# High and low parts side by side in the inputs of two feed-forward layers

## The chip, the core and the metric

The kernel runs on one core of one Trainium2 chip. The metric is the device time of one execution in microseconds (us); lower is better. Engines carry the profile's names: PE is TensorE's matmul, PEld its weight load, DVE is VectorE, ACT ScalarE, POOL GpSimd, SP SyncE. In a matmul the stationary side is loaded into the array first (a LDWEIGHTS, shown under PEld), and the moving side then streams past it; the number of moving columns is the last number of a row's 128x512.

## The reference

A decoder trunk of two layers over 256 positions of width 2048, all in float32. Cut to what matters here:

```python
D_MODEL, SEQ, DEPTH = 2048, 256, 2
D_FF = (8 * D_MODEL + 3 * 256 - 1) // (3 * 256) * 256      # 5632

def rms_norm(x, g):
    xf = x.astype(jnp.float32)
    y = xf * lax.rsqrt(jnp.mean(xf * xf, axis=-1, keepdims=True) + NORM_EPS)
    return (y * g.astype(jnp.float32)).astype(x.dtype)

def swiglu(x, w_gate, w_up, w_down):
    return (jax.nn.silu(x @ w_gate) * (x @ w_up)) @ w_down

def reference(x, ...):
    for layer in range(DEPTH):
        xn = rms_norm(x, norm_mix[layer])
        if layer % 2 == 0:
            x = x + mixer_mlstm_ssd(xn, *mixer_params[layer])
        else:
            x = x + mixer_moba(xn, *mixer_params[layer])
        x = x + swiglu(rms_norm(x, norm_ffn[layer]), *ffn_params[layer])
    return rms_norm(x, final_norm)
```

The change touches the input of `swiglu` in both layers, and nothing of the two mixers.

## The kernel before

**Precision.** A matmul takes float32r operands. To keep float32 accuracy each operand is split into a high part (the value rounded to float32r) and a low part (what is left over), and a product of two operands is three matmuls: high by high, high by low, low by high (`add`, L470 to L474).

**Activations.** A `KT` (L256) holds one activation matrix, transposed: 2048 features are 16 k-tiles of 128, in four blocks of four k-tiles, each block a tile `[P, 4, 2, T]` of 128 partitions, four k-tiles, high and low, and 256 positions. So the high part of a k-tile is a run of 256 values of four bytes, and its low part the next run. `parts(k)` gives the two views, `both(k)` both as one run of 512 columns, which only the strips of `lin_w` use as a moving side. `x1` and `x3` are the inputs of the feed-forward layers, `x2` that of the attention; `normed_later` (L924) makes all three. The gain of the norm is folded into the split (`turned`, L286): PE transposes 128 x 128 pieces of the residual into PSUM, ACT writes the high part and DVE the low part. The norm's factor per position is put in after the matmuls.

**Weights.** `weights` (L427) loads the rows of one pair of k-tiles, 128 x 2 x 512 values from each of two sources, and splits them: ACT writes `wh`, DVE subtracts and writes `wl`.

**Strips.** `block` (L456) computes 256 positions by two strips of 512 columns; for gate and up one strip of each. It walks the 16 k-tiles as eight pairs, in an order that a plan gives, a letter for each pair. At a `P` it issues the plain product: four outputs (two halves of the positions by two strips), two k-tiles, three matmuls, 24 in all. At an `S` the pair, seen as a 2 x 2 block matrix, goes by a scheme with seven products in place of eight (21 matmuls), for which sums and differences of weights (`sums`, `sh`, `sl`) and of activations (`kt.sums`, made by `activation_sums`, L308) are needed. The activation sums are split into high and low too; their tiles are `skx`, `[P, 4, 2, P]`, four sums of 128 positions. In all these matmuls the activations (128 positions of a k-tile or of a sum) are the stationary side and the 512 weight columns the moving one.

**The feed-forward layer.** `ffn` (L992) handles its 5632 hidden columns as 11 strips in groups of 4, 4 and 3. For each strip `hidden` runs a `block` of gate and up over `x1` or `x3`; the first strip's plan is `PLAN_LATE`, PPPSPSPP, that of the others `PLAN_X`, PSPSPSPP. The hidden values are transposed and split into a `KT` `ha` or `hb`, and after each group `add_blocks` multiplies them by the down weights and adds them to the residual. So each value of `x1` and `x3` is written once and loaded by 11 strips, the values of `ha` and `hb` by the two column halves of one down product.

**Order.** A tile framework sets semaphores and puts instructions in order by priority; nothing in it depends on the step of an operand. All weights come through the SP queue, 512 KB at a time.

Of the kernel before, what the change touches and what calls it, by code (L numbers as in the profile page):

```python
# [9 lines left out]
F32 = mybir.dt.float32  # L10
F32R = mybir.dt.float32r
# [6 lines left out]
P = 128  # L18
T = 256
NT = T // P  # L20
D = 2048
KD = D // P
# [43 lines left out]
def hybrid_trunk(ctx: ExitStack, tc: tile.TileContext, a: dict, out: bass.AP):  # L66
    nc = tc.nc
# [83 lines left out]
    def small(shape, name, dt=F32):  # L151
        return res.tile(shape, dt, tag="small", name=name, bufs=PLAN_X.count("S"))
# [103 lines left out]
    class KT:  # L256


        def __init__(self, name, n, home=blk):
            self.name, self.blocks, self.home, self.sums = name, [None] * (n // 4), home, {}  # L260

        def block(self, b):
            if self.blocks[b] is None:
                self.blocks[b] = self.home([P, 4, 2, T], f"{self.name}{b}", F32R)
            return self.blocks[b]

        def parts(self, k):
            need((self.name, k // 4))
            b = self.block(k // 4)
            return b[:, k % 4, 0, :], b[:, k % 4, 1, :]  # L270

        def both(self, k):
            need((self.name, k // 4))
# [10 lines left out]
            turned(kt, b, pt.rearrange("p (a b) -> p a b", a=2), gcol, half)  # L284

    def turned(kt, b, pair, gcol, half):  # L286
        blk_ = kt.block(b)
        ks = slice(2 * half, 2 * half + 2)
        summed = 2 * b + half in kt.sums
        if summed:  # L290
            xg = t2([P, 2, T], "xg")
            if gcol is None:
                nc.scalar.copy(xg, pair)
            else:
                for j in range(2):
                    c = gcol + 4 * b + 2 * half + j
                    nc.scalar.activation(xg[:, j, :], pair[:, j, :], AF.Copy, scale=pv[:, c:c + 1])
            split(blk_[:, ks, 0, :], blk_[:, ks, 1, :], xg)
            kt.sums[2 * b + half] = activation_sums(xg, gcol is not None)
        elif gcol is None:  # L300
            split(blk_[:, ks, 0, :], blk_[:, ks, 1, :], pair)
        else:
            for j in range(2):
                k = 2 * half + j
                split(blk_[:, k, 0, :], blk_[:, k, 1, :], pair[:, j, :],
                      pv[:, gcol + 4 * b + k:gcol + 4 * b + k + 1])

    def activation_sums(a, gains):  # L308

        a11, a12, a21, a22 = a[:, 1, :P], a[:, 0, :P], a[:, 1, P:], a[:, 0, P:]  # L310
        sf = t2([P, 4, P], "sf")
        nc.vector.tensor_add(sf[:, 0, :], a21, a22)
        nc.vector.tensor_sub(sf[:, 2, :], a11, a21)
        nc.vector.tensor_sub(sf[:, 1, :], sf[:, 0, :], a11)
        nc.vector.tensor_sub(sf[:, 3, :], a12, sf[:, 1, :])
        if gains:
            sk = small([P, 4, 2, P], "skx", F32R)
        else:
            sk = held_tile("skh", [P, 4, 2, P], "skh", F32R)
        split(sk[:, :, 0, :], sk[:, :, 1, :], sf)  # L320
        return sk

    def sums_of(kt, j):

        need((kt.name, j // 2))
        pair = kt.block(j // 2)[:, 2 * (j % 2):2 * (j % 2) + 2, :, :]
        xg = t2([P, 2, T], "xg")
        nc.vector.tensor_add(xg, pair[:, :, 0, :].bitcast(F32), pair[:, :, 1, :].bitcast(F32))
        kt.sums[j] = activation_sums(xg, True)

    def transpose_later(kt, b, src, gcol, wait, step=1):
        for half in range(2):
# [123 lines left out]
    def block(src, kt, row, nk, plan, after_sums=None, lead=1, pairs=None, ahead=()):  # L456

        n = nk // 2
        pairs = pairs[:plan.count("S")] if pairs else [j for j in range(n) if plan[j] == "S"]
        rest = [j for j in range(n) if j not in pairs]
        order = [(pairs if kind == "S" else rest).pop(0) for kind in plan]
        F = [None] * 4
        pre = None
        E = {}

        def add(dst, a, b, start, stop):  # L470
            (ah, al), (bh, bl) = a, b
            nc.tensor.matmul(dst, ah, bh, start=start, stop=False)  # L472
            nc.tensor.matmul(dst, ah, bl, start=False, stop=False)  # L473
            nc.tensor.matmul(dst, al, bh, start=False, stop=stop)  # L474

        first_s, last_s = plan.find("S"), plan.rfind("S")
        turn["aux"] = 0
        group = []
        for i_, j in enumerate(order):
            for when, fn, *args in ahead:  # L480
                if when == i_:
                    fn(*args)
            for i in range(i_, min(i_ + 3, n)):
                if plan[i] == "S" and order[i] not in kt.sums:
                    sums_of(kt, order[i])
            if plan[i_] == "S":
                held[0] = True
                wh, wl, sh, sl = weights(src, row + 2 * j * P, True)
                tok = lambda k, t: tuple(x[:, t * P:(t + 1) * P] for x in kt.parts(k))
                k2, k1 = 2 * j, 2 * j + 1  # L490
                a11, a12, a22 = tok(k1, 0), tok(k2, 0), tok(k2, 1)
                sk = kt.sums[j]
                s1, s2, s3, s4 = [(sk[:, i, 0, :], sk[:, i, 1, :]) for i in range(4)]
                b21, b11, b22 = [(wh[:, i, :], wl[:, i, :]) for i in range(3)]
                t3, t1, t2_, t4 = [(sh[:, i, :], sl[:, i, :]) for i in range(4)]
                prod = {1: (a11, b11), 2: (a12, b21), 3: (s4, b22), 4: (a22, t4),
                        5: (s1, t1), 6: (s2, t2_), 7: (s3, t3)}
                for p in (2, 3, 1, 7, 5, 6, 4):
                    if p in (2, 3, 4):
                        i = p - 2  # L500
                        add(F[i], *prod[p], start=False, stop=False)
                    else:
                        if p not in E:
                            E[p] = bank({1: 4, 7: 5, 5: 6, 6: 7}[p], "acc_e")
                        add(E[p], *prod[p], start=i_ == first_s, stop=i_ == last_s)
                if i_ == last_s:
                    pre = [t2([P, STRIP], "pre") for _ in range(4)]
                    p1, v, u3, w = pre
                    with tc.high_priority(offset=1600 if lead == 1 else 400):
                        nc.scalar.copy(p1, E[1])  # L510
                        nc.vector.tensor_add(v, p1, E[6])
                        nc.vector.tensor_add(u3, v, E[7])
                        nc.vector.tensor_add(v, v, E[5])
                        nc.vector.tensor_add(w, u3, E[5])
                        if after_sums is not None:
                            after_sums(pre)
            else:
                group.append((j, weights(src, row + 2 * j * P, False)))
                if len(group) < lead and i_ < n - 1 and n - i_ <= lead:
                    continue  # L520
                for i in range(4):
                    t, s = divmod(i, 2)
                    first = F[i] is None
                    if first:
                        F[i] = bank(i, "acc_f")
                    for cut in halved if len(group) == lead == 2 and i == 3 else (slice(0, STRIP),):
                        for jj, (wh, wl) in group:
                            for kk in range(2):
                                xh, xl = kt.parts(2 * jj + kk)
                                ts = slice(t * P, (t + 1) * P)  # L530
                                add(F[i][:, cut], (xh[:, ts], xl[:, ts]), (wh[:, 2 * s + kk, cut], wl[:, 2 * s + kk, cut]),
                                    start=first and jj == group[0][0] and kk == 0,
                                    stop=jj == order[-1] and kk == 1 and cut.stop == STRIP)
                group = []
            tick()
            if i_ == last_s:
                held[0] = False
        return F, pre
# [384 lines left out]

    def normed_later(name, gcol, waits=((2, 1), (2, 1), (1, 0), (2, 0))):  # L924

        nx = KT("x" + name, KD, long)
        nx.sums = summed(PLAN_X)
        ss = cst.tile([P, NT, 4], F32, name="ss" + name)

        def finish(s):  # L930
            cs = slice(s * STRIP, (s + 1) * STRIP)
            transpose_later(nx, s, [xr_[t][:, cs] for t in range(NT)], gcol, *waits[s])
            for t in range(NT):
                sumsq(ss[:, t, s:s + 1], xr_[t][:, cs])

        return nx, ss, finish
# [260 lines left out]
```

## Time and profile before

| | |
|---|---|
| Time, median of 2 runs | 2580.02 us (2579.95 to 2580.09) |
| Span of the profiled execution, first to last instruction | 2578.2 us |
| Matmuls, and as many weight loads | 12222 |
| Moved by DMA | 496.55 MB, 193 GB/s on average |
| Groups that read `x` as stationary side in `block`: L472, L473, L474 on acc_f | 1122 matmuls each |

The profile is one execution, taken by the hardware's profiler. Its page lists busy time by engine, the span in 40 slices, the DMA queues, the chain of work that ended last, and the costliest groups of instructions: source line, engine, operation, written tile, read tiles, shape, count, then busy time in us, mean duration in ns, and the idle time of the engine just before them with what ended it. The durations of matmuls overlap, since they are pipelined and their ends are modelled (a row of 390 ns can follow another by 227 ns), so distances are taken from start to start. In the view of the order in time a row has the start in us, the duration, the engine, and at its end how many equal instructions it stands for. In the view of one tile a row has minimum, median and maximum duration in ns, then the first and the last start in us.

### The profile page before, as it was taken

What the parts mean: (1) busy time and instruction counts of PE and PEld (TensorE: products, weight loads), DVE (VectorE), ACT (ScalarE), POOL (GpSimd) and SP (SyncE); (2) the same over time, 40 slices, a digit from 0 to 9 for tenths busy, and PEclk for the clock granted to TensorE, in tenths of its full rate; (3) what the DMA queues carried; (4) which work ended last, traced back from release to release, by engine and by line L of the source; (5) the groups of instructions that cost most, each with busy time, mean ns of one, the idle gap of its engine ahead of it and who ended that gap; (6) DMA issues with size and microseconds to landing.
All of it is one profiled execution on the core that took longest, in us unless ns stands there. A gap on an engine that the chain in (4) does not pass through costs nothing.

```text
span 2578.2 us, 32660 instructions
## 1 busy us (share of the span) xinstructions
PE 2563.5 (99%) x12222; PEld 2130.7 (83%) x12222; DVE 2196.5 (85%) x2831; ACT 1454.3 (56%) x1929; POOL 43.6 (2%) x77
## 2 busy tenths in 40 slices
PE   9999999999999999999999999999999999999998
PEld 8888888888888888888888888888888888888887
DVE  6676777799989998899889986767999888988898
ACT  6465665566665554555455665666655545554554
POOL 2000010000000000000000000000000000000000
PEclk9999999999999999999999999999999999999999
DMA  7566576566564656465656556554555655565554
GB/s 237 170 211 182 166 235 182 163 205 212 185 213 163 215 194 212 163 226 188 206 167 225 186 174 229 164 180 146 180 192 200 212 181 199 193 213 191 199 188 154
DMA packets 254767, 496.55 MB, mean 193 GB/s; under 512 B 15704, under 2 KB 16608, under 8 KB 254352
## 3 DMA queue, kind: packets, MB, share of 16 engines
q1 hardware_dynamic: 250384, 483.26, 57.1%
q0 software_dynamic: 2896, 8.51, 1.1%
q10 hardware_dynamic: 1328, 2.70, 0.3%
q8 instruction: 96, 1.57, 0.2%
q14 instruction: 63, 0.52, 0.1%
HBM read 492.26 MB, written 2.14 MB: 192 GB/s over the span
## 4 chain that ended last, share of the span: by engine, by line
PE 90%; DVE 5%; issue 2%; DMA 2%; ACT 1%; SPq 0%; POOL 0%; POOLq 0%; DVEq 0%; ACTq 0%
PE acc_f L473 18%; PE acc_f L474 18%; PE acc_f L472 17%; PE acc_w L381 11%; PE acc_w L385 5%; PE acc_e L472 4%; PE acc_e L473 4%; PE acc_e L474 4%; PE acc_a L412 2%; PE acc_a L413 2%; PE acc_a L411 2%; DVE wl L441 2%; PE p_tr L282 2%; PE p_y L866 1%; DMA raw<-in_l_w_o 1%
## 5 line engine op out<-in xcount | busy, mean ns | idle before, releaser
L439 ACT CAST wh<-raw 128x1024 fp32r<-128x1024 f32 (+1 forms) x577 | 630.0, 1134 | 412.9 <-PE acc_f L474 338.1
L441 DVE TENSOR_TENSOR wl<-raw,wh 128x1024 fp32r<-128x1024 f32 (+1 forms) x577 | 748.7, 1323 | 79.1 <-ACT wh L439 73.8
L474 PE MATMUL acc_f<-wh,x 128*128 128x512 f32 x1122 | 438.2, 391 | 0.0
L473 PE MATMUL acc_f<-wl,x 128*128 128x512 f32 x1122 | 437.5, 390 | 0.1
L472 PE MATMUL acc_f<-wh,x 128*128 128x512 f32 x1122 | 436.5, 391 | 0.0
L366 DVE TENSOR_TENSOR wl<-raw,wh 128x1024 fp32r<-128x1024 f32 (+1 forms) x225 | 271.3, 1218 | 139.8 <-ACT wh L365 137.3
L439 ACT CAST wh<-sums 128x1024 fp32r<-128x1024 f32 x222 | 227.9, 1051 | 225.9 <-PE acc_f L474 137.7
L365 ACT CAST wh<-raw 128x1024 fp32r<-128x1024 f32 (+1 forms) x225 | 231.9, 1044 | 196.3 <-PE acc_w L381 111.6
L441 DVE TENSOR_TENSOR wl<-sums,wh 128x1024 fp32r<-128x1024 f32 x222 | 266.7, 1221 | 34.6 <-ACT wh L439 34.1
L473 PEld LDWEIGHTS acc_f<-wl,x 128*128 128x128 f32 x1122 | 210.7, 188 | 44.9 <-DVE wl L441 1.9
L474 PEld LDWEIGHTS acc_f<-wh,x 128*128 128x128 f32 x1122 | 210.7, 188 | 43.1
L472 PEld LDWEIGHTS acc_f<-wh,x 128*128 128x128 f32 x1122 | 210.6, 188 | 42.6
L381 PE MATMUL acc_w<-xa,wh 128*128 128x512 f32 x768 | 207.5, 398 | 1.5 <-DVE xa L229 1.5
L381 PEld LDWEIGHTS acc_w<-xa,wh 128*128 128x128 f32 x768 | 138.8, 189 | 27.9 <-DVE xa L229 1.6
L448 DVE TENSOR_TENSOR sums<-raw 128x1024 f32<-128x1024 f32 x111 | 135.4, 1220 | 12.9 <-DMA raw<-in_l_ffn_up 8.0
L381 PE MATMUL acc_w<-x,wh 128*128 128x512 f32 x512 | 138.9, 399 | 0.0
L385 PE MATMUL acc_w<-xa,wl 128*128 128x256 f32 x768 | 121.8, 282 | 0.0
L385 PEld LDWEIGHTS acc_w<-xa,wl 128*128 128x128 f32 x768 | 110.1, 190 | 6.7
L474 PE MATMUL acc_f<-wh,hb 128*128 128x512 f32 (+1 forms) x284 | 109.6, 387 | 0.0
L473 PE MATMUL acc_f<-wl,hb 128*128 128x512 f32 (+1 forms) x284 | 109.6, 387 | 0.0
L472 PE MATMUL acc_f<-wh,hb 128*128 128x512 f32 (+1 forms) x284 | 109.5, 387 | 0.0
L472 PE MATMUL acc_f<-wh,ha 128*128 128x512 f32 x280 | 109.0, 390 | 0.0
(362 smaller groups left out, 4581.3 us busy)
## 6 DMA issues: line engine op xcount, KB each, us to landing
raw<-in_l_w_in SPq DMA_DIRECT2D x191, 512.0 KB, 3.7
raw<-in_l_ffn_gate SPq DMA_DIRECT2D x176, 512.0 KB, 3.9
raw<-in_l_ffn_up SPq DMA_DIRECT2D x176, 512.0 KB, 4.8
raw<-in_l_ffn_down SPq DMA_DIRECT2D x176, 512.0 KB, 5.2
raw<-in_l_w_qkv SPq DMA_DIRECT2D x96, 512.0 KB, 4.7
raw<-in_l_w_out SPq DMA_DIRECT2D x64, 512.0 KB, 5.2
raw<-in_l_w_o SPq DMA_DIRECT2D x32, 512.0 KB, 4.9
rows<-scr POOLq DMA_DIRECT2D x10, 512.0 KB, 5.2
```

Of the source, the lines that this page charges most:

```text
L282: nc.tensor.transpose(pt[:, j * T + t * P:j * T + (t + 1) * P], src[t][:, c:c + P], ident)
L365: nc.scalar.copy(wh[:, ks, :], raw[:, ks, :])
L366: nc.vector.tensor_sub(wl[:, ks, :], raw[:, ks, :], wh[:, ks, :].bitcast(F32))
L381: return nc.tensor.matmul(banks[f], wh[:, kk, f * P:(f + 1) * P], kt.both(k0 + kk), start=k0 + kk == 0, stop=False, skip_group_check=True)
L385: nc.tensor.matmul(banks[f][:, :T], wl[:, kk, f * P:(f + 1) * P], kt.parts(k0 + kk)[0], start=False, stop=k0 + kk == nk - 1, skip_group_ch ...
L411: nc.tensor.matmul(banks[t], xh[:, ts], wh[:, kk, :], start=k0 + kk == 0, stop=False)
L439: nc.scalar.copy(h[:, c, :], of[:, c, :])
L441: nc.vector.tensor_sub(l[:, c, :], of[:, c, :], h[:, c, :].bitcast(F32))
L448: nc.vector.tensor_sub(sums[:, 0:2, :], raw[:, 2:4, :], raw[:, 3:0:-2, :])
L472: nc.tensor.matmul(dst, ah, bh, start=start, stop=False)
L473: nc.tensor.matmul(dst, ah, bl, start=False, stop=False)
L474: nc.tensor.matmul(dst, al, bh, start=False, stop=stop)
```

## The change

`KT` gets a flag `paired`. With it a block has the shape `[P, 4, T, 2]`: the high and the low part of one value lie next to each other, and each of the two views (`half`) is a run of 256 values at a step of two. `activation_sums` does the same with its tile, `[P, 4, P, 2]`. The flag is set for `x1` and `x3`; all other activations keep their layout. Sizes and places of all tiles stay as they were. The views of TensorE's stationary side, of ACT's and DVE's writes, and of DVE's read of the high part while it makes the low one, have a step of two elements; all instructions stand in the same order on every engine as before.

```diff
-        def __init__(self, name, n, home=blk):
-            self.name, self.blocks, self.home, self.sums = name, [None] * (n // 4), home, {}
+        def __init__(self, name, n, home=blk, paired=False):
+            self.name, self.blocks, self.home, self.sums, self.paired = name, [None] * (n // 4), home, {}, paired
 
         def block(self, b):
             if self.blocks[b] is None:
-                self.blocks[b] = self.home([P, 4, 2, T], f"{self.name}{b}", F32R)
+                shape = [P, 4, T, 2] if self.paired else [P, 4, 2, T]
+                self.blocks[b] = self.home(shape, f"{self.name}{b}", F32R)
             return self.blocks[b]
+
+        def half(self, b, ks, i):
+            return self.block(b)[:, ks, :, i] if self.paired else self.block(b)[:, ks, i, :]
 
         def parts(self, k):
             need((self.name, k // 4))
-            b = self.block(k // 4)
-            return b[:, k % 4, 0, :], b[:, k % 4, 1, :]
+            return self.half(k // 4, k % 4, 0), self.half(k // 4, k % 4, 1)
...
     def turned(kt, b, pair, gcol, half):
...
-            split(blk_[:, ks, 0, :], blk_[:, ks, 1, :], xg)
-            kt.sums[2 * b + half] = activation_sums(xg, gcol is not None)
+            split(kt.half(b, ks, 0), kt.half(b, ks, 1), xg)
+            kt.sums[2 * b + half] = activation_sums(xg, gcol is not None, kt.paired)
...
-                split(blk_[:, k, 0, :], blk_[:, k, 1, :], pair[:, j, :],
+                split(kt.half(b, k, 0), kt.half(b, k, 1), pair[:, j, :],
                       pv[:, gcol + 4 * b + k:gcol + 4 * b + k + 1])
...
+        shape = [P, 4, P, 2] if paired else [P, 4, 2, P]
         if gains:
-            sk = small([P, 4, 2, P], "skx", F32R)
+            sk = small(shape, "skx", F32R)
         else:
-            sk = held_tile("skh", [P, 4, 2, P], "skh", F32R)
-        split(sk[:, :, 0, :], sk[:, :, 1, :], sf)
+            sk = held_tile("skh", shape, "skh", F32R)
+        sk = [sk[:, :, :, i] if paired else sk[:, :, i, :] for i in range(2)]
+        split(sk[0], sk[1], sf)
         return sk
...
-                s1, s2, s3, s4 = [(sk[:, i, 0, :], sk[:, i, 1, :]) for i in range(4)]
+                s1, s2, s3, s4 = [(sk[0][:, i, :], sk[1][:, i, :]) for i in range(4)]
...
-        nx = KT("x" + name, KD, long)
+        nx = KT("x" + name, KD, long, name in ("1", "3"))
```

More of the change, by code (lines that the diff above doesn't have):

```diff
@@ L286, in turned @@
     def turned(kt, b, pair, gcol, half):
-        blk_ = kt.block(b)
         ks = slice(2 * half, 2 * half + 2)
@@ L297, in turned @@
                     nc.scalar.activation(xg[:, j, :], pair[:, j, :], AF.Copy, scale=pv[:, c:c + 1])
-            split(blk_[:, ks, 0, :], blk_[:, ks, 1, :], xg)
-            kt.sums[2 * b + half] = activation_sums(xg, gcol is not None)
+            split(kt.half(b, ks, 0), kt.half(b, ks, 1), xg)
+            kt.sums[2 * b + half] = activation_sums(xg, gcol is not None, kt.paired)
         elif gcol is None:
-            split(blk_[:, ks, 0, :], blk_[:, ks, 1, :], pair)
+            split(kt.half(b, ks, 0), kt.half(b, ks, 1), pair)
         else:
@@ L304, in turned, with activation_sums @@
                 k = 2 * half + j
-                split(blk_[:, k, 0, :], blk_[:, k, 1, :], pair[:, j, :],
+                split(kt.half(b, k, 0), kt.half(b, k, 1), pair[:, j, :],
                       pv[:, gcol + 4 * b + k:gcol + 4 * b + k + 1])
-    def activation_sums(a, gains):
+    def activation_sums(a, gains, paired=False):
         a11, a12, a21, a22 = a[:, 1, :P], a[:, 0, :P], a[:, 1, P:], a[:, 0, P:]
@@ L325, in sums_of @@
         need((kt.name, j // 2))
-        pair = kt.block(j // 2)[:, 2 * (j % 2):2 * (j % 2) + 2, :, :]
+        ks = slice(2 * (j % 2), 2 * (j % 2) + 2)
         xg = t2([P, 2, T], "xg")
-        nc.vector.tensor_add(xg, pair[:, :, 0, :].bitcast(F32), pair[:, :, 1, :].bitcast(F32))
-        kt.sums[j] = activation_sums(xg, True)
+        nc.vector.tensor_add(xg, kt.half(j // 2, ks, 0).bitcast(F32), kt.half(j // 2, ks, 1).bitcast(F32))
+        kt.sums[j] = activation_sums(xg, True, kt.paired)
     def transpose_later(kt, b, src, gcol, wait, step=1):
```

## The prediction, made before the changed kernel ran

> **What bounds the kernel now.** I read the page's table of engines first, then its slices and its chain of work, then the stretches in which the feed-forward layers read their input, and last the order in time of the matmuls and weight loads inside one of them.
>
> ```profile
> span 2578.2 us, 32660 instructions
> PE 2563.5 (99%) x12222; PEld 2130.7 (83%) x12222; DVE 2196.5 (85%) x2831; ACT 1454.3 (56%) x1929; POOL 43.6 (2%) x77
> ...
> PEclk9999999999999999999999999999999999999999
> ...
> PE 90%; DVE 5%; issue 2%; DMA 2%; ACT 1%; SPq 0%; POOL 0%; POOLq 0%; DVEq 0%; ACTq 0%
> ```
>
> TensorE (PE) is busy 99% of the span, its clock is granted in full, and 90% of the chain that ended last are its matmuls. No other engine can hand back much; a change helps or hurts by what it does to the distance from one matmul to the next. The busy time of PE counts overlapping, modelled ends, so I go by starts.
>
> The six rows below are the stretches in which gate and up strips read `x1` (the first three) and `x3`, with their sum. The columns are the length, then the busy time of PE, PEld, DVE, ACT and POOL, the clock, and the DMA share and rate.
>
> ```profile
> 775.10:947.90 172.80, 172.70 (x776) 140.99 (x775) 161.79 (x196) 99.96 (x117) 0.70 (x1) 1.00 0.57 190
> 1033.60:1203.70 170.10, 170.10 (x758) 138.75 (x758) 154.23 (x170) 93.34 (x98) 0.00 (x0) 1.00 0.57 194
> 1289.40:1416.60 127.20, 127.18 (x566) 104.03 (x565) 115.69 (x128) 69.97 (x73) 0.00 (x0) 1.00 0.58 198
> 1862.80:2035.60 172.80, 172.80 (x777) 140.83 (x776) 161.81 (x193) 101.02 (x118) 0.70 (x1) 1.00 0.57 191
> 2121.30:2291.30 170.00, 170.00 (x757) 138.74 (x756) 154.08 (x170) 93.33 (x98) 0.00 (x0) 1.00 0.58 193
> 2377.10:2504.90 127.80, 127.29 (x567) 104.01 (x566) 115.65 (x128) 70.14 (x73) 0.00 (x0) 1.00 0.59 197
> sum 940.70, PE 940.07 PEld 767.35 DVE 863.24 ACT 527.76 POOL 1.39; mean PE 156.68 PEld 127.89 DVE 143.87 ACT 87.96 POOL 0.23
> ```
>
> The change can act on 940.7 us of the span. PE fills them, but VectorE (DVE) is close behind: 161.8 of 172.8 us (94%) in the first stretch, 154.2 of 170.1 (91%) in the second.
>
> Inside the first layer's gate and up strips the order in time shows 28 matmuls in a row; I quote the first and the last, and of the loads the first and the last as well.
>
> ```profile
> 899.66 0.39 PE L474 MATMUL acc_f<-wh,x 128*128 128x512 f32 x1
> ...
> 905.78 0.39 PE L474 MATMUL acc_f<-wh,x 128*128 128x512 f32 x1
> ...
> 899.89 0.19 PEld L473 LDWEIGHTS acc_f<-wl,x 128*128 128x128 f32 x1
> ...
> 905.78 0.19 PEld L472 LDWEIGHTS acc_f<-wh,x 128*128 128x128 f32 x1
> ```
>
> 27 steps in 6.12 us: 226.7 ns from matmul to matmul, and one load for each. So the matmuls in question cost 226.7 ns apiece, and 4032 of them (counted below) make 914 us of those 940.7.
>
> How much of the 226.7 ns belongs to the load? Three more rows say something about it: eight matmuls of 256 columns, 24 of 64 columns, and eight of 512 columns that use the weights as the stationary side.
>
> ```profile
> 445.14 1.12 PE L385 MATMUL acc_w<-xa,wl 128*128 128x256 f32 x8
> 437.82 2.79 PE L866 MATMUL p_y<-y,dec 128*128 128x64 f32 x24
> 443.30 2.00 PE L381 MATMUL acc_w<-xa,wh 128*128 128x512 f32 x8
> ```
>
> ```profile
> L385 PE MATMUL acc_w<-xa,wl 128*128 128x256 f32 x768 | 121.8, 282 | 0.0
> L866 PE MATMUL p_y<-y,dec 128*128 128x64 f32 x192 | 24.0, 271 | 0.1
> ```
>
> Taking one duration off each stretch: 256 columns go at (1.12 - 0.28) / 7 = 120 ns, 64 columns at (2.79 - 0.27) / 23 = 110 ns. A matmul of 64 columns is far shorter than that, so 110 ns is what a load of 128 contiguous columns takes when nothing else holds it up. And 226.7 - 120 = 106.7 ns for 256 columns more, so 512 columns alone are 213.3 ns, and 13.3 ns of each matmul do not depend on its columns. This fixed part is where a load can cost even while it is hidden. It isn't quite constant: the last of the three rows gives (2.00 - 0.39) / 7 = 230 ns.
>
> **The change part by part.** All three edits (the block's shape, the sums' shape, the views into both) do one thing: within a tile of the same size, high and low parts of a value become neighbours. The built program has the same instructions in the same order on every engine; no wait, DMA, pool or semaphore is added, and no queue is passed. What differs is the step of operands.
>
> *Loads.* A strip walks 16 k-tiles in eight pairs. A plain pair issues 4 x 2 x 3 = 24 matmuls, a summed one 7 x 3 = 21. With the plan PSPSPSPP a strip has 5 x 24 + 3 x 21 = 183, with PPPSPSPP 186; each layer has one strip of the second kind and ten of the first. 2 x (186 + 10 x 183) = 4032 loads now pick every second element out of 1,024 bytes per partition where they read 512 contiguous bytes. The trace of before has no such load, so its price has to be bounded from rows. If the load alone slows down by a factor f, it takes 110 f ns, which stays under a matmul's 226.7 ns up to f = 2.06; a load of half the speed, 220 ns, is still covered by the matmul ahead of it. What then remains is the fixed part of 13.3 ns: at best it goes to nothing (4032 x 13.3 ns = -53.8 us), and if it follows the bytes that a load spans it doubles (+53.8 us). I take it as unchanged, since the nearest row, a load of equally many columns beside an equal matmul, is the one measured at 226.7 ns, and the column count, not the bytes, is what stays the same. Term: 0, ends -53.8 and +53.8 us.
>
> [...]
>
> *Writes.* Each of `x1` and `x3` is written by ten pairs of ACT and DVE instructions of 256 columns and three of 512, and its sums by three more of 512.
>
> ```profile
> L228 ACT ACTIVATE x<-p_tr,pv x30: 460/474/500, 769.0 to 1878.5; 128x256 fp32r<-128x256 f32 x30
> L229 DVE SCALAR_TENSOR_TENSOR x<-p_tr,pv,x x30: 475/479/485, 769.5 to 1879.4; 128x256 fp32r<-128x256 f32 x30
> L225 ACT CAST x<-xg x9: 610/622/650, 771.2 to 1873.2; 128x512 fp32r<-128x512 f32 x9
> L226 DVE TENSOR_TENSOR x<-xg,x x9: 681/687/695, 773.6 to 1873.9; 128x512 fp32r<-128x512 f32 x9
> L225 ACT CAST skx<-sf x20: 605/618/622, 518.4 to 1874.8; 128x512 fp32r<-128x512 f32 x20
> L226 DVE TENSOR_TENSOR skx<-sf,skx x20: 682/685/693, 519.5 to 1877.0; 128x512 fp32r<-128x512 f32 x20
> ```
>
> (The counts also hold `x2`, and the sums of other inputs.) Per layer that is 10 x 0.479 + 3 x 0.687 + 3 x 0.685 = 8.9 us on DVE and 10 x 0.474 + 3 x 0.622 + 3 x 0.618 = 8.5 us on ACT. They now write, and DVE also reads, every second element. The work per element stays, which excludes a gain. Were each twice as slow, DVE would spend 2 x 8.9 = 17.8 us more in all, all of it around the start of a layer, where it has little room; ACT, at 100.0 of 172.8 us, would hide its own. The nearest row with an unusual order is the first of these two, which reads its rows backwards at a step of two rows:
>
> ```profile
> L448 DVE TENSOR_TENSOR sums<-raw 128x1024 f32<-128x1024 f32 x111 | 135.4, 1220 | 12.9 <-DMA raw<-in_l_ffn_up 8.0 <-DMA raw<-in_l_w_o 1.7 <-DMA raw<-in_l_w_out 1.6
> L441 DVE TENSOR_TENSOR wl<-sums,wh 128x1024 fp32r<-128x1024 f32 x222 | 266.7, 1221 | 34.6 <-ACT wh L439 34.1
> ```
>
> 1220 ns against 1221 ns in plain order. So I take 1 us, with ends 0 and 17.8. What covers it: PE has other strips' matmuls before it while the blocks are written. Without that cover the wait would stand on the first reads of `x` in a strip, and of the split weights queued behind on DVE.
>
> *Sum.* 2578.2 + 0 + 1 = 2579.2 us of span; the timed runs' median of 2580.02 us is 1.8 us above that span, so 2581 us.
>
> **The rivals.** *The fixed part shrinks.* For it: the 13.3 ns aren't rigid, as 230 ns beside 226.7 shows, so loads and matmuls seem to get into each other's way, and another rhythm of the loads can suit better. Against it: a load that spans more bytes has no plain reason to disturb less. Halved, it gives 4032 x 6.7 = 27 us less, 2553 us; gone altogether, 2526 us, but then the first stretch shrinks by 5.9% (13.3 of 226.7) to 162.6 us, with 161.8 us of DVE work in it: DVE would be the bound there, and a part would be given back as waits for split weights.
>
> *The fixed part grows with the bytes spanned.* This one ends on the other side. It acts on each of the 4032 matmuls; doubled to 26.7 ns the pace is 240 ns, +53.8 us, 2634 us, and it is slower by more than 2% once the pace gains 51.6 us / 4032 = 12.8 ns. For it: the excess exists and varies with how loads and matmuls meet. Against it: nothing in the rows ties the 13.3 ns to bytes rather than to the 128 columns of a load, and those stay.
>
> *The load becomes the bound.* If a strided load is more than 2.06 times slower, matmuls wait for weights: at 2.5 times, 275 - 226.7 = 48.3 ns x 4032 = +195 us, 2775 us. Against it: the row of 110 ns leaves a factor of two; for it: nothing in the trace has ever loaded at a step.
>
> That the change isn't carried out is no rival: the built program has 4032 stationary operands at a step of two.
>
> **How the numbers follow.** Unchanged pace: 42%, at 2581 us, and 5% more for writes that surface, up to 2598 us. The shrinking fixed part: 25%, 2526 to 2570 us. The growing one: 20%, 2590 to 2636 us. Load-bound: 8%, above that. I take 2581 us, and a range from 2536 to 2636 us: it leaves out the load-bound case and the far ends of the two next to it, together about 15 to 20%. About 2% (51.6 us) is what a measurement of this kernel can tell from no change. Faster than 2528.4 us needs nearly all of the fixed part gone in spite of DVE: 3%. Slower than 2631.6 us is the load-bound case and half of the growing one: 18%. Within 2%: 79%.
>
> **What would show each step.** In the first layer's gate and up strips the start-to-start distance should stay at 226.7 ns; 213 to 224 ns means that the fixed part shrank, about 240 ns that it follows the bytes, and loads that take well over 190 ns with matmuls 250 ns or more apart mean that the load is the bound. L228, L229, L225 and L226 on `x` and `skx` should keep 474, 479, 620 and 686 ns. The down strips, which read `ha` and `hb`, must stay at 226.7 ns. The prediction is wrong if the six stretches change by more than a few us in sum, or if the time moves while their pace does not.

## The result, and the profile after

| | before | after |
|---|---|---|
| Time, median of 2 runs | 2580.02 us | 2601.47 us (2601.29 to 2601.66) |
| Ratio, 95% interval | | 1.0083 (1.0053 to 1.0112) |
| Span of the profiled execution | 2578.2 us | 2599.5 us |

The changed kernel takes 21.45 us more, 0.83%. That is within 2%, and inside the range of 2536 to 2636 us; but the likeliest case was a pace that doesn't move, and it did. By the prediction's own sign of being wrong, six stretches that change by more than a few us in sum, its mechanism failed: they changed by 21.9 us.

The page of the kernel after: the span, the table of engines, the granted clock and the chain of work.

```profile
span 2599.5 us, 32660 instructions
PE 2587.1 (100%) x12222; PEld 2156.3 (83%) x12222; DVE 2198.3 (85%) x2831; ACT 1454.9 (56%) x1929; POOL 43.5 (2%) x77
...
PEclk9999999999999999999999999999999999999999
...
PE 92%; DVE 4%; DMA 2%; issue 2%; ACT 1%; SPq 0%; POOL 0%; POOLq 0%; ACTq 0%; DVEq 0%
```

Same instructions, same clock. PE's busy time is 23.6 us longer and PEld's 25.6, those of DVE and ACT by less than 2. So the time came on TensorE itself.

The first of the six stretches in which gate and up strips read their input, and the sum of all six (length, busy PE, PEld, DVE, ACT, POOL, clock, DMA share and rate; in the sum, busy times alone):

```profile
774.90:951.30 176.40, 176.40 (x777) 145.37 (x776) 162.26 (x196) 100.13 (x117) 0.70 (x1) 1.00 0.55 187
...
sum 962.60, PE 962.26 PEld 791.42 DVE 865.73 ACT 528.91 POOL 1.39; mean PE 160.38 PEld 131.90 DVE 144.29 ACT 88.15 POOL 0.23
```

962.6 - 940.7 = 21.9 us: the six stretches hold the whole difference. Inside one of them, the matmuls in order of time (start, length, engine, line; lines stand four further down than before, so L476 is the old L472):

```profile
922.41 0.39 PE L476 MATMUL acc_f<-wh,x 128*128 128x512 f32 x1
...
925.90 0.39 PE L476 MATMUL acc_f<-wh,x 128*128 128x512 f32 x1
```

15 steps in 3.49 us: 232.7 ns where it was 226.7. The rows of the tile `x` (lowest, median and highest duration in ns), of a load before:

```profile
L472 PEld LDWEIGHTS acc_f<-wh,x x1122: 186/188/192, 774.9 to 2504.0; 128*128 128x128 f32 x187
```

and after, with the writes:

```profile
L476 PEld LDWEIGHTS acc_f<-wh,x x1122: 186/193/201, 774.6 to 2525.3; 128*128 128x128 f32 x187
L476 PE MATMUL acc_f<-wh,x x1122: 389/394/491, 774.9 to 2525.5; 128*128 128x512 f32 x187
...
L228 ACT ACTIVATE x<-p_tr,pv x30: 463/493/532, 768.8 to 1888.5; 128x256 fp32r<-128x256 f32 x30
L229 DVE SCALAR_TENSOR_TENSOR x<-p_tr,pv,x x30: 470/476/485, 769.3 to 1889.4; 128x256 fp32r<-128x256 f32 x30
L225 ACT CAST x<-xg x9: 620/664/698, 770.9 to 1883.2; 128x512 fp32r<-128x512 f32 x9
L226 DVE TENSOR_TENSOR x<-xg,x x9: 680/683/693, 773.3 to 1883.9; 128x512 fp32r<-128x512 f32 x9
```

A load beside a matmul is 193 ns long in the median (188 before), a matmul 394 (389). The writes are as good as unmoved on DVE (476 and 683 ns after 479 and 687) and 4 to 7% longer on ACT (493 and 664 after 474 and 622), which has time to spare. All starts of matmuls in the six stretches, counted from the traces by what follows:

```
matmul to matmul, start to start        before              after
closer than 260 ns                      3909 in 888.0 us    3922 in 915.6 us   (227.2 -> 233.4 ns)
260 ns apart or more (a late start)       87 in  28.1 us      71 in  23.3 us
transposes, and the step up to one       197 in  24.9 us     197 in  23.4 us
sum                                            941.0 us            962.3 us
```

So each of 4032 matmuls costs 6.3 ns more, 25.4 us, and some 4 us come back, for the most part because late starts get rarer (28.1 us become 23.3). A slower TensorE seems to wait less. The view of waits shows it over the whole span at another place, the transposes of the hidden values, which wait for DVE; before:

```profile
PEld p_tr L282 <- DVE h L1012: 8.6, 31, 0.5
```

and after (us in all, times, longest):

```profile
PEld p_tr L285 <- DVE h L1016: 5.4, 25, 0.3
```

### The profile page after: what moved, and what is told of

The parts are those of the page before. It is cut to its first block, busy times and chain, and to the rows that moved or that the text cites. A ratio compares the mean times of both kernels' runs of the same rounds, so it can differ in the third digit from the quotient of the medians.

```text
span 2599.5 us, 32660 instructions
## 1 busy us (share of the span) xinstructions
PE 2587.1 (100%) x12222; PEld 2156.3 (83%) x12222; DVE 2198.3 (85%) x2831; ACT 1454.9 (56%) x1929; POOL 43.5 (2%) x77
## 4 chain that ended last, share of the span: by engine, by line
PE 92%; DVE 4%; DMA 2%; issue 2%; ACT 1%; SPq 0%; POOL 0%; POOLq 0%; ACTq 0%; DVEq 0%
PE acc_f L478 18%; PE acc_f L477 18%; PE acc_f L476 18%; PE acc_w L385 11%; PE acc_w L389 5%; PE acc_e L476 4%; PE acc_e L477 4%; PE acc_e L478 4%; PE acc_a L416 2%; PE acc_a L417 2%; PE acc_a L415 2%; PE p_tr L285 1%; DVE wl L445 1%; PE p_y L870 1%; DMA raw<-in_l_w_o 1%
## 5 line engine op out<-in xcount | busy, mean ns | idle before, releaser
L478 PE MATMUL acc_f<-wh,x 128*128 128x512 f32 x1122 | 443.3, 395 | 0.0
L476 PE MATMUL acc_f<-wh,x 128*128 128x512 f32 x1122 | 441.5, 396 | 0.0
L443 ACT CAST wh<-sums 128x1024 fp32r<-128x1024 f32 x222 | 227.5, 1049 | 233.2 <-PE acc_f L478 147.1
L369 ACT CAST wh<-raw 128x1024 fp32r<-128x1024 f32 (+1 forms) x225 | 231.8, 1044 | 195.8 <-PE acc_w L385 111.5
L477 PEld LDWEIGHTS acc_f<-wl,x 128*128 128x128 f32 x1122 | 216.4, 193 | 45.6 <-DVE wl L445 1.3
L478 PEld LDWEIGHTS acc_f<-wh,x 128*128 128x128 f32 x1122 | 216.5, 193 | 43.7
L476 PEld LDWEIGHTS acc_f<-wh,x 128*128 128x128 f32 x1122 | 216.4, 193 | 43.3
L476 PE MATMUL acc_f<-wh,hb 128*128 128x512 f32 (+1 forms) x284 | 109.5, 387 | 0.0
```

The costliest lines, as they stand in the source:

```text
L369: nc.scalar.copy(wh[:, ks, :], raw[:, ks, :])
L443: nc.scalar.copy(h[:, c, :], of[:, c, :])
```

## The experiments

What was open: 6.3 ns per matmul is neither of the two prices the prediction had for a change (13.3 ns more, or 6.7 to 13.3 less). Is a load at step two slower, does VectorE or ScalarE get in its way, does it follow the bytes spanned, and is it the step at all?

**Loads at several steps, with nothing beside them.** A kernel of its own: rows of 48 matmuls, each with its own load, stationary side at step 1, 2, 3, 4 and 8, or at step one from shifted starts (`sshift`, elements 2 + 136 i), at 512, 256 and 128 moving columns, with DVE and ACT at rest.

```diff
+    def view(name, i):
+        if name == "shift":
+            lo = 2 + 136 * (i % 8)
+            return st[name][:, lo:lo + P]
+        n = {"one": 1, "two": 2, "three": 3, "four": 4, "eight": 8}[name]
+        lo = (i // n) % (D // (n * P)) * n * P + i % n
+        return st[name][:, lo:lo + n * (P - 1) + 1:n]
```

> A kernel of its own that computes nothing of the trunk: it hands the input through and otherwise only runs rows of 48 float32r matmuls, whose stationary side of 128 columns is read at a step of 1, 2, 3, 4 and 8 elements, and at a step of 1 that begins two elements off, each beside 512, 256 and 128 moving columns. Read are the start-to-start distances. Theory S (what a load takes from its neighbour grows with the bytes that it spans): at 512 columns 226.7, 233.3, 240, 246.7 and 273 ns for the steps 1, 2, 3, 4, 8, and 226.7 for the shifted one. Rival A (any step other than 1 costs the same 6.7 ns): 226.7 at step 1, 233.3 at all others. Rival L (a load itself gets slower with the step and the matmul waits for the rest): at 256 and 128 columns the distance grows with the step well above 120 ns, and at 512 columns it stays flat until the load is longer than the matmul. Rival W (the loss needs the writing or reading of VectorE and ScalarE beside it, which are idle here): all about 213 ns at 512 columns.

The order in time on PE, a row for each 48 matmuls; from one row's start to the next row's start, by 48, is the pace:

```profile
33.05 11.36 PE L45 MATMUL acc<-mv,stwo 128*128 128x512 f32 x48
44.26 11.46 PE L45 MATMUL acc<-mv,sthree 128*128 128x512 f32 x48
55.55 11.45 PE L45 MATMUL acc<-mv,sfour 128*128 128x512 f32 x48
66.84 11.92 PE L45 MATMUL acc<-mv,seight 128*128 128x512 f32 x48
78.59 11.31 PE L45 MATMUL acc<-mv,sshift 128*128 128x512 f32 x48
89.74 5.92 PE L45 MATMUL acc<-mv,sone 128*128 128x256 f32 x48
...
101.25 8.58 PE L45 MATMUL acc<-mv,sthree 128*128 128x256 f32 x48
109.67 11.37 PE L45 MATMUL acc<-mv,sfour 128*128 128x256 f32 x48
120.87 11.72 PE L45 MATMUL acc<-mv,seight 128*128 128x256 f32 x48
...
138.11 5.47 PE L45 MATMUL acc<-mv,sone 128*128 128x128 f32 x48
143.42 5.82 PE L45 MATMUL acc<-mv,stwo 128*128 128x128 f32 x48
149.07 9.51 PE L45 MATMUL acc<-mv,sthree 128*128 128x128 f32 x48
```

Step two at 512 columns: (44.26 - 33.05) / 48 = 233.5 ns, the changed kernel's own pace, with DVE and ACT at rest; they are not the cause. At 128 columns step one gives (143.42 - 138.11) / 48 = 110.6 ns, where 64 columns went at 110 in the kernel before, so the load is the bound there; step two gives 117.7. At 256 columns steps three and four give 175.4 and 233.3 ns, far over the 120 ns of step one. So a load by itself loses 6% at step two, and half its speed only at step four. The load is not the bound at step two; yet the pace rises. Steps three and four at 512 columns give 235.2 ns both, (55.55 - 44.26) / 48 and (66.84 - 55.55) / 48, little more than step two: not the 240 and 246.7 of theory S, and nearest to rival A (only step eight has more, 244.8). From the shifted starts at step one it was (89.74 - 78.59) / 48 = 232.3 ns at 512 columns, which I had not expected and took up below. (In the rows of 128 columns from step three on the granted clock fell from 1.00 to 0.50, so they are left out.)

**Each half of the change alone.** `x1` and `x3` at step two with their sums plain (3264 loads), and the sums alone (768 loads). Against the changed kernel, the first and the second:

```diff
-            kt.sums[2 * b + half] = activation_sums(xg, gcol is not None, kt.paired)
+            kt.sums[2 * b + half] = activation_sums(xg, gcol is not None)
...
-        kt.sums[j] = activation_sums(xg, True, kt.paired)
+        kt.sums[j] = activation_sums(xg, True)
```

```diff
-                shape = [P, 4, T, 2] if self.paired else [P, 4, 2, T]
+                shape = [P, 4, 2, T]
...
-            return self.block(b)[:, ks, :, i] if self.paired else self.block(b)[:, ks, i, :]
+            return self.block(b)[:, ks, i, :]
```

> Only x1 and x3 have their parts side by side, their sums keep the old layout: 3264 of the 4032 loads have a step of two. If the time comes from the loads alone, each costing the same, it takes 3264/4032 of the 21.4 us: 2597.4 us, with 233.3 ns where x is loaded and 226.7 ns where the sums are. Rival: a good part comes from strided writes around the start of a layer; then the share is not that of the loads.

> Only the sums of x1 and x3 have their parts side by side: 768 of the 4032 loads. Loads alone: 768/4032 of 21.4 us = 4.1 us, 2584.1 us. Rival, neighbours matter: a row of matmuls that changes between steps of one and two at every third matmul finds no common rhythm, and the cost per load lies well above 6.7 ns, 2590 us or more.

Measured: 2598.45 us for the first (kernel before beside it 2581.09; ratio 1.0069, interval 1.0054 to 1.0084) and 2584.92 us for the second (1.0017, 1.0007 to 1.0026): +17.4 and +3.8 us, together 21.2 of the 21.45. That is 5.3 and 5.0 ns per load. So the loss goes by the number of loads at step two, in the rows of `x` as in those of the sums.

**Step four.** The parts of two k-tiles interleaved, and those of two sums: four values side by side, each picked at a step of four.

```diff
-                shape = [P, 4, T, 2] if self.paired else [P, 4, 2, T]
+                shape = [P, 2, T, 4] if self.paired else [P, 4, 2, T]
...
+                return self.block(b)[:, ks // 2, :, 2 * (ks % 2) + i]
...
```

> The parts of two k-tiles are interleaved (high, low, high, low), so every load of x1, x3 and their sums has a step of four and spans 2,048 bytes. Theory S: 246.7 ns per matmul, 20 ns more than before, 4032 x 20 = 81 us, 2661 us less what idle time takes up. Rival A: as the changed kernel, 2601 us. Rival L, a load of half the speed or less: above 220 ns a load, so 2601 us to 2800 us, with distances that follow the load and not the matmul. The writes are at a step of four too: where ACT or DVE slow down it shows in their rows.

2618.75 us, ratio 1.0147 (1.0132 to 1.0162). The tile's rows, of a load and of two writes:

```profile
L485 PEld LDWEIGHTS acc_f<-wh,x x1122: 186/310/338, 775.2 to 2541.3; 128*128 128x128 f32 x187
...
L225 ACT CAST x<-xg x9: 621/1124/1195, 772.0 to 1894.2; 128x512 fp32r<-128x512 f32 x9
L226 DVE TENSOR_TENSOR x<-xg,x x9: 685/1114/1136, 774.8 to 1895.4; 128x512 fp32r<-128x512 f32 x9
```

The load is 310 ns long beside a matmul (193 at step two) and the writes now do take 1.6 to 1.8 times as long; the matmuls' distance is about 235 ns in the mean, what the small kernel gives at step four. There the load alone takes 233.3 ns, more than the 226.7 of a matmul, so it may be the bound by now; but the small kernel's step three has the same 235.2 ns with a load of 175.4, so the pace alone does not show it. Doubling the bytes spanned once more added some 2 ns: a price by bytes, with its 240 ns at step two and 246.7 at step four, is refuted.

**What about the load sets the price.** The same small kernel in rows of 42, with 128, 96, 64 or 32 stationary columns, 512 down to 256 moving columns, and starts of either side some elements on.

```diff
+            w = s[:, lo:lo + step * (rows - 1) + 1:step]
+            m = moff + (i % 2) * 1024
+            tc.keep_in_program_order(nc.tensor.matmul(banks[i % 4][:rows, :n], w, mv[:, m:m + n], start=True, stop=True))
```

> Again nothing of the trunk is computed, only rows of 42 float32r matmuls run, each with its own load. First 128, 96, 64 and 32 stationary columns beside 512 moving ones, at step one and step two; then 512, 448, 384, 320 and 256 moving columns; then stationary starts 0, 1, 2, 3, 4, 8 and 16 elements off at step one, 0 and 1 at step two, and moving starts 0, 1, 2, 4 and 8 elements off; then the same stationary slice again and again; at the end the plain case. Theory S2 (the fixed part goes with the bytes that a load spans, at up to 1,024 bytes): 64 columns at step two span as much as 128 at step one and lose the same 13.3 ns (226.7), 64 at step one lose less. Theory C (it goes with the columns loaded, a bit more at a step): 128, 96, 64, 32 columns lose 13.3, 10, 6.7 and 3.3 ns at step one, 20, 15, 10 and 5 at step two. Theory F (a fixed change-over for each load, whatever its length): 226.7 in all of them at step one. Theory B (places of the two operands clash): the distance changes with the start of the stationary or the moving side, and some start falls well below 226.7.

Three rows and what follows each, in order of time:

```profile
42.83 9.68 PE L45 MATMUL acc<-mv,sa 128*128 128x512 f32 x42
52.35 9.83 PE L45 MATMUL acc<-mv,sb 128*96 128x512 f32 x42
...
202.82 9.92 PE L45 MATMUL acc<-mv,sb 128*128 128x512 f32 x42
212.58 9.85 PE L45 MATMUL acc<-mv,sa 128*128 128x512 f32 x42
...
290.44 10.10 PE L45 MATMUL acc<-mv,sa 128*128 128x512 f32 x42
300.38 9.96 PE L45 MATMUL acc<-mv,sb 128*128 128x512 f32 x42
```

By start to start: 128 columns at step one 9.52 / 42 = 226.7 ns; step one with the stationary side one element on (202.82) 232.4; with the moving side one element on (290.44) 236.7. The mean distances with each row's first twelve matmuls left out:

```
ns, 512 moving columns      stationary columns  128    96     64     32
  step one                                      226.7  230.1  229.8  231.8
  step two                                      233.3  230.6  226.7  226.7
stationary start, elements on (step one)   0: 226.7  1: 232.3  2: 230.6  3: 229.8  4: 233.4  8: 233.3
moving start, elements on (step one)       0: 226.7  1: 236.6  2: 233.3  4: 231.6  8: 233.3
128 stationary columns, moving columns          512    448    384    320    256
  step one                                      226.7  202.5  173.3  146.7  120.0
  step two                                      233.3  203.4  173.3  146.6  120.0
```

At step one fewer stationary columns don't make a load cheaper (231.8 ns at 32, 226.7 at 128): neither a price by bytes nor one by columns holds, and a fixed price for each load doesn't either. From 384 moving columns down, step two costs nothing. At step two the pace was 233.3 from start 0 and from one element on alike, so it is not the low parts' odd start that costs. And at 512 moving columns a load at step one costs as much as one at step two if either side starts elsewhere. The step is one way among several to lose the 226.7.

**Which starts are good.** Rows of 30, both starts in steps of 32 elements (128 bytes) at step one, and finer at step two; then rows of 36 with the stationary start 0, 2, ... 62 elements on, at either step.

```diff
+    for off in (0, 32, 64, 128):
+        for moff in (0, 32, 64, 128):
+            run(512, 1, off=off, moff=moff)
+    for off in (0, 4, 8, 16, 32, 64):
+        for moff in (0, 4, 8, 16, 32, 64):
+            run(512, 2, off=off, moff=moff)
...
+    for off in range(0, 64, 2):
+        run(512, 1, off=off)
```

> Nothing of the trunk is computed; rows of 30 float32r matmuls of 512 columns. 16 rows at step one: stationary starts 0, 32, 64 and 128 elements off, each with moving starts 0, 32, 64 and 128 elements off. 36 rows at step two: both starts 0, 4, 8, 16, 32 and 64 elements off. Theory P (the 6.7 ns of step two are a matter of where the operands start, as the 6.7 ns of a start 4, 8 or 16 elements off at step one are): some pairs of starts give 226.7 ns at step two, and starts by whole 32 elements keep 226.7 at step one. Rival R (step two loses it wherever the operands lie): every row at step two at 233.3 ns or more. If a pair at step one falls clearly below 226.7 ns, it would be a gain for the whole kernel.

> Nothing of the trunk is computed; rows of 36 float32r matmuls of 512 columns whose stationary side starts 0, 2, 4, ... 62 elements behind the moving side (modulo 64 elements, 256 bytes), at step one and then at step two. Theory P (the distance depends on the difference of the two starts within 256 bytes, since 64 behaved as 0): step one stays at 226.7 at 0 only and lies between 229 and 234 elsewhere, step two at 233.3 at 0 and 229.9 at 16, with a pattern of its own between. Rival R2 (229.9 at 16 was a passing rhythm): step two scatters around 233 without a pattern. A start that falls clearly below 226.7 at either step would be a version worth running.

Of the first of the two, step one with the moving side 0 and then 32 elements on (34.79 and 41.59), step two with both starts equal (144.85), and with the stationary side 16 elements (64 bytes) on (270.60):

```profile
34.79 6.96 PE L45 MATMUL acc<-mv,sa 128*128 128x512 f32 x30
41.59 7.16 PE L45 MATMUL acc<-mv,sb 128*128 128x512 f32 x30
48.58 6.98 PE L45 MATMUL acc<-mv,sa 128*128 128x512 f32 x30
...
144.85 7.16 PE L45 MATMUL acc<-mv,sa 128*128 128x512 f32 x30
151.85 7.16 PE L45 MATMUL acc<-mv,sb 128*128 128x512 f32 x30
...
270.60 7.06 PE L45 MATMUL acc<-mv,sa 128*128 128x512 f32 x30
277.49 7.16 PE L45 MATMUL acc<-mv,sb 128*128 128x512 f32 x30
```

6.80 / 30 = 226.7, 6.99 / 30 = 233.0, 7.00 / 30 = 233.3 and 6.89 / 30 = 229.7 ns. In all 16 rows at step one the pace was 226.7 where the two starts are equal modulo 64 elements (256 bytes), and 232.7 to 233.6 where they differ by 32. At step two it lay between 229.9 and 233.6, never at 226.7; with equal starts it was 233.3 at 0 and 231.1 four elements on. The finer rows were no smooth curve: at step one 226.7 at 0, but also at 30 and 54, and 228.3 to 234.1 elsewhere; at step two 230.0 at 18, 26 and 28. 16 elements on gave 229.9 in the first kernel and 233.3 in the second, so what a row settles into also hangs on something other than the difference of the starts; what ran ahead of it is one candidate that no run tests. No row in either kernel was under 226.6. I had hoped for one: that would have been a version to beat the kernel before.

In the kernel before, all matmuls of `block` have both starts equal modulo 256 bytes, by the addresses of the built program. That can be taken away without touching a step.

**Placement alone, at step one.** The kernel before, with a filler tile ahead of the buffers shortened by 128 bytes, so that half of the activations' tiles (`x1`, `x3` and their sums among them) start 128 bytes off the weights, modulo 256.

```diff
-    pad2.tile([P, 40], F32, name="pad2")
+    pad2.tile([P, 8], F32, name="pad2")
```

> The kernel before with the spare tile pad2 32 elements shorter: every operand keeps its step of one, but x1, x3, their sums, x2, xa and half of my now start 128 bytes off the weights, modulo 256. Theory P: 233.5 ns in the six gate and up stretches, as at step two, so 22 us more there, and about 7 ns more for each of some 2,300 other block and lin_a matmuls on xa, x2, my and sums, 16 us: 2615 to 2625 us, while the down products stay at 226.7. Rival, the step itself is what costs: 2580 us, no change.

2607.58 us, ratio 1.0108 (1.0092 to 1.0124), with not one load at step two. The six stretches' sum:

```profile
sum 959.20, PE 958.82 PEld 770.46 DVE 865.84 ACT 528.78 POOL 1.39; mean PE 159.80 PEld 128.41 DVE 144.31 ACT 88.13 POOL 0.23
```

959.2 - 940.7 = 18.5 us, nearly what the change costs there (21.9), at a mean distance of 232.6 ns; the other 9 us lie outside, with the other tiles that moved (matmuls on `xa` went from 227.5 to 232.7 ns). The down strips, whose operands still have equal starts, stayed at 227.2. My figure of 2615 to 2625 us was too high; the rival, that it would cost nothing, was wrong altogether.

**The changed kernel, placed better.** Step two as in the change, with the filler 64 bytes shorter: the small kernel's best case at step two.

```diff
-    pad2.tile([P, 40], F32, name="pad2")
+    pad2.tile([P, 24], F32, name="pad2")
```

> The changed kernel with pad2 16 elements shorter: x1, x3 and their sums keep their step of two and start 64 bytes behind the weights modulo 256. Theory P: 229.9 ns in place of 233.3 in the six stretches, 3.4 ns x 4032 = 14 us less than the 962.6 us there, about 949 us. xa, x2 and half of my, at step one and 64 bytes off, get slower elsewhere (6 to 7 ns for some 2,300 matmuls, 15 us), so the time in all stays near 2600 us. Rival R2: the six stretches keep 962 us or more.

2597.57 us, ratio to before 1.0068 (1.005 to 1.0086). The stretches:

```profile
sum 952.70, PE 952.29 PEld 795.35 DVE 865.63 ACT 528.79 POOL 1.39; mean PE 158.72 PEld 132.56 DVE 144.27 ACT 88.13 POOL 0.23
```

952.7 us: about half of the 21.9 comes back there (230.4 ns per matmul), as foreseen within 4 us; some of it is lost again outside, where tiles at step one were displaced too.

**More loads at step two.** The changed kernel with `ha`, `hb` and `skh` side by side as well, 2028 loads more.

```diff
-            hT = KT(f"h{name}{first}", 4 * n)
+            hT = KT(f"h{name}{first}", 4 * n, blk, True)
```

> The changed kernel with the two parts of ha, hb and skh side by side too, so that the down blocks' 1740 loads of h parts and the 288 loads of skh's parts are also taken at a step of two: 2028 loads more, beside the 4032 of the changed kernel. If each matmul beside a load at step two costs the same wherever it stands (6.3 ns more, as the 4032 showed), the time rises by 2028 x 6.3 = 12.8 us less the few that late starts give back: 2612 to 2614 us, and the pace of the down strips goes from 227.1 to about 233 ns. If the extra cost belonged to the gate and up blocks alone (their sums, their stream from the weights' queue, their two banks), the down strips would stay at 227 ns and the time at 2601 to 2603 us. If the writes at step two on ScalarE and VectorE, which are on the path at the down strips' starts, matter too, the time goes above 2615 us.

2614.54 us, ratio to before 1.0127 (1.0109 to 1.0145): 13.1 us over the changed kernel's 2601.47, in another batch whose kernel before was 1.9 us slower; less that, 11.2 us of the 12.8 foreseen. The loads of `ha` (188 ns in the median until now):

```profile
L476 PEld LDWEIGHTS acc_f<-wh,ha x280: 193/193/201, 951.3 to 1498.2; 128*128 128x128 f32 x140
```

The down strips' mean distance went from 227.1 to 233.6 ns, by 6.5 ns where the gate and up strips' rose by 6.3. So the cost belongs to the loads, and not to the gate and up strips, their two banks or their streams of weights.

## Why the prediction came out as it did

**What bounds the kernel:** right. PE was and is the bound, and the six stretches (940.7 to 962.6 us) hold the whole difference.

**Loads: the term that was mis-sized.** It was taken as 0 and measured 25.4 us, of which some 4 come back through rarer late starts. It lies inside the ends of -53.8 and +53.8 us, about half-way from 0 to the upper one. The step that failed reads "the column count, not the bytes, is what stays the same": it made 226.7 ns a property of the two operands' sizes. The runs showed that it is the best case of equal sizes: 226.7 when both start at the same place modulo 256 bytes at step one, mostly 228 to 237 when a start, the step or the number of stationary columns is another. All of the block's matmuls were in the best case, so the profile of before had little but 226.7 in those rows (93% of the distances lie between 224 and 229 ns), and the single hint (230 ns at L381) went to the rivals alone. Where that hint comes from is open. It is not a difference of starts, for those operands have equal ones; rows of 512 and 256 moving columns alternate there, and no run tests whether that matters. Nor is the fixed part the same at all widths: 213.3 + 13.3 came from two rows, and at 448 columns the small kernel gave 202.5 ns, where that line would give 200.

The bound on the load itself held: at step two it takes 117.7 ns alone against 110.6 at step one, factor 1.06, far from 2.06; step four, with 233.3 ns in the rows of 256 columns, is the first past that. What didn't follow is that a hidden load of nearly full speed costs nothing.

**Writes:** right. 1 us was taken; DVE kept its 476 and 683 ns, ACT took 19 to 42 ns more for each, about 1 us in all and covered.

**The rivals.** The fixed part shrank nowhere at 512 moving columns. It grew, but not with the bytes spanned: step four spans twice the bytes of step two and cost some 2 ns more. The load as the bound is shown only from step three on, in the small kernel at 256 columns. So the direction was the second rival's, the size half of its 53.8 us, and its reason wrong.

**Sum and range:** 2581 us was 20.5 us short, 0.8%. The range held because its ends came from what the 13.3 ns could do at most; that the time lies in it is in part luck, since the case that it fell into had 20% and a reason that the runs refute.

**What stays open.** Why equal starts modulo 256 bytes are the good case, and what else makes a row settle at 226.7, 230 or 233.3, isn't settled. The pace moves with either side's start (232.4 ns with the stationary side one element on, 236.7 with the moving side), but no run shows what joins the two. And no row of the small kernels went clearly below 226.7 ns at 512 columns.

## What to carry to other kernels

A weight load that is fully hidden under a matmul can still cost (here 6.3 ns for each of 4032 matmuls): judge a change to its operand by the start-to-start distance of the matmuls beside it, not by the load's own duration. Where every matmul sits at the same lowest distance, take that as a best case that a new step or a new start address can spoil, here by 3%, and keep the two operands' starts equal modulo 256 bytes at step one: with 128 stationary and 512 moving columns that gave 226.7 ns in every such row of the small kernels from the second on, though some other starts (30 and 54 elements on) did too. An edit that only changes a tile's size can move everything allocated behind it: compare addresses before blaming the edit itself.

## What the hardware showed that I had not expected

- A tile placed 128 bytes off, at step one, costs as much per matmul as a step of two: 232.6 against 233.4 ns; the whole kernel before became 27.6 us slower by a filler of other length.
- A load of fewer columns is not a cheaper one: with 32 stationary columns at step one a pace of 231.8 ns, with 128 one of 226.7.
- The loss vanishes with fewer moving columns: at 384, 320 and 256 the pace is 173.3, 146.7 and 120.0 ns at either step.
- Writes of ACT and DVE at a step of two elements of four bytes cost 0 to 7% more, at a step of four 1.6 to 1.8 times as much.
